# Modulation rows of a two-layer decoder trunk: row sums turned on VectorE, running sums pinned in the traced order, an earlier fold

## The chip, the cores and the metric

The kernel runs on one core of one Trainium2 chip. The metric is the device time of one execution in microseconds (us), as the median of several runs; lower is better. One execution is also recorded by the hardware profiler, and all rows below are from that one. Engines: PE is TensorE (matmul), PEld its weight loads, DVE is VectorE, ACT is ScalarE, POOL is GpSimd, SP is SyncE, which here only issues DMA transfers.

## The reference, cut to what matters

The trunk has two layers over a sequence of 512 tokens and a width D of 2048: first differential attention (8 heads), then forgetting attention (16 heads), which reads keys and values projected once from the first layer's output ("shared"). Each mixer reads its input modulated by a conditioning vector c:

```python
c_act = jax.nn.silu(c)                                   # 2048 numbers
mod = c_act @ w_mod[l] + b_mod[l]                        # 2048 x 6144 for each layer
shift, scale, gate = jnp.split(mod, 3, axis=-1)
h = x * (1.0 + scale[:, None]) + shift[:, None]
y = diff_attention(h, ...)                               # layer 0; forgetting_attention in layer 1
x = layer_norm(DN_ALPHA * x + gate[:, None] * y, ln_g[l], ln_b[l])
# between the layers, for the shared keys and values:
mod = c_act @ w_mod_kv + b_mod_kv                        # 2048 x 4096
shift, scale = jnp.split(mod, 2, axis=-1)
hk = x * (1.0 + scale[:, None]) + shift[:, None]
```

The change concerns the rows `c_act @ w` that are not needed at the start: the gate of layer 0, shift and scale of the shared projection ("kv"), and shift, scale and gate of layer 1, which are six rows of 2048 numbers.

## The kernel before, in words

**Projections.** All big products are done as three products of float32r parts (a value is split into a rounded "high" part and the remainder, "low"; `products`, lines 171 to 175: high x high, high x low, low x high). `group` (line 302) makes one projection of 512 columns: it holds four PSUM banks (`acc`), walks over 8 weight tiles, and for each tile issues four "bursts", one for each bank, of 6 matmuls with 512 moving columns. A `WeightStream` loads each weight tile (`wst`), ACT writes its high part (`whi`, line 93), DVE its low part (`wlo`, line 94), three tiles deep. When a bank's sum is complete, an `evac` function takes it out of PSUM through ACT and DVE; the next group writes the same bank.

**Order.** After each burst `tick` (line 286) runs one entry of the list `pieces` (a step of a head's attention, or nothing) and then, if the group's `bg` says so, takes the next step of a generator, `background`. The instructions are traced in this order. A scheduler then fixes the order on each engine when the context ends: it may move an instruction ahead of others traced before it, when its inputs are ready by the scheduler's own reckoning. Engines run their own instructions strictly in the order so fixed.

**Stages.** First comes a start stage (to about 200 us) with layer 0's own shift and scale and heads 0 and 1. Then come the groups of heads 2 to 7 in pairs: queries and keys (`qk[h]`), values and gate (`vg[h]`). While head h is projected, the attention of head h-1 runs as pieces: scores, softmax on DVE and ACT, transposes, values, and a norm that ends in `og` (line 758), whose transposes on PE are at line 772. The `evac` of a `vg` group writes `vl` (line 169) and `sg` (line 678). In `vg[7]` DVE also splits the finished heads into `hl`. Then the first output projection (`oA`, four groups of 512 columns), the shared values (`vj`) and keys (`kj`), layer 1's projections with its attention, and the second output projection.

**Later modulation.** `mod_stream` (line 353) is the generator in `background`. A row of 2048 numbers is made in four segments of 512 columns. For each segment 16 tiles of 128 x 512 weights are loaded (`ms`, two tiles to a 512 KB load, two buffers; in layer 1 single tiles `ms` and `msk`), and DVE adds them up: `macc = w * cact[:, kt] + macc`, one instruction for a step of the generator (line 387 for the first tile, 389 for the others), two `macc` buffers. That leaves 128 partial sums for each column, one for each partition, which must be added across partitions. `mod_row` (line 399) does that: ACT and DVE split `macc` into `mhi` and `mlo` (lines 168, 169), two PE matmuls with a matrix of ones as the stationary operand (lines 409, 410) add over the partitions into the bank `tr`, DVE adds the bias (`mrow`, line 411), and a DMA writes the 512 numbers to DRAM. The split is traced with tile 1 of the next segment, the matmuls with its tile 5. Segments 0 to 15 (line 633) run under the heads: gate of layer 0, kv shift, kv scale, layer 1's shift; 8 more (line 1106) under the shared projections. Steps are taken from `qk[3]` on (`bg=lambda k: k % 3 > 0`, then `k % 4 > 0`), one for each burst in the first `oA` group, and what is left in `open_n` (line 923).

**Fold.** `fold` (line 941) reads a finished pair of rows back from DRAM, turns it on PE (line 944) and merges it with the layer norm's parameters. For kv it is called in `open_n`, at the first bank's end in the first `oA` group.

Of the kernel before, what the change touches and what calls it, by code (L numbers as in the profile page):

```python
# [2 lines left out]

# [106 lines left out]
def tile_yoco(  # L110
# [50 lines left out]
    def tr_bank(name="tr"):  # L161
        return ps.tile([P, 512], F32, name=name, tag="tr", bufs=1)
# [4 lines left out]
    def split(hi, lo, src):  # L167
        S.copy(hi, src)
        V.tensor_tensor(lo, src, hi.bitcast(F32), op=ALU.subtract)
# [132 lines left out]
    def group(job, natural, evac, banks=range(4), bg=0, before_sub=None, after_sub=None, hold=0, after_held=None):  # L302


        acc = {b: acc_bank() for b in banks}
        w = job.width
        count = 0
        ns = KT // 2

        def burst(s, b, hi, lo):  # L310
            nonlocal count
            for kk in range(2):
                kt = 2 * s + kk
                bs = slice(b * P, (b + 1) * P)
                start, stop = kt == 0, kt == KT - 1
                if natural:
                    products(acc[b][:, :w], (Hh[kt][:, bs], Hl[kt][:, bs]), (hi[kk][:, :w], lo[kk][:, :w]), start, stop)
                else:
                    products(acc[b], (hi[kk][:, bs], lo[kk][:, bs]), (Hh[kt], Hl[kt]), start, stop)
            if s == ns - 1:  # L320
                evac(b, acc[b])
            tick(bg(count) if callable(bg) else bg)
            count += 1

        for s in range(ns - hold):
            if before_sub:
                before_sub(s)
            hi, lo = ws.get(job, s)
            for b in banks:
                burst(s, b, hi, lo)  # L330
            if after_sub:
                after_sub(s)
        for s in range(ns - hold + 3, ns):
            ws.advance(ws.where[(id(job), s)])

            pool, tag = (kpool, "K") if s < ns - hold + 5 else (hpool, "H")
            ws.step(lambda: pool.tile([P, 512], F32R, name="held", tag=tag))
# [15 lines left out]
    def mod_stream(segs, new_stage, new_acc, nk, deep=0, new_deep=None):  # L353

        todo = [(i, r) for i in range(len(segs)) for r in range(KT // nk)]
        loaded = {}
        summed = []

        def load(k):
            i, r = todo[k]
            src, col, _ = segs[i]
            t = new_deep() if k < deep else new_stage()
            rows = src[nk * r * P : nk * (r + 1) * P, col : col + 512]
            nc.sync.dma_start(t, rows.rearrange("(k p) n -> p k n", p=P) if nk > 1 else rows)
            loaded[k] = t

        def load_upto(k):
            n = len(loads)  # L370
            while n < len(todo) and n <= (k + 7 if n < deep else k + 2 // nk):
                load(n)
                loads.append(n)
                n += 1

        loads = []
        load_upto(-1)
        for k, (i, r) in enumerate(todo):
            load_upto(k)
            if r == 0:  # L380
                acc = new_acc()
            t = loaded.pop(k)
            for kk in range(nk):
                kt = nk * r + kk
                w = t[:, kk, :] if nk > 1 else t
                if kt == 0:
                    V.tensor_scalar(acc, w, cact[:, 0:1], None, op0=ALU.mult)
                else:
                    V.scalar_tensor_tensor(acc, w, cact[:, kt : kt + 1], acc, op0=ALU.mult, op1=ALU.add)  # L389
                if kt == KT - 1:  # L390
                    summed.append(segs[i][2](acc))
                if kt in (1, 5) and summed:
                    if next(summed[0], None) is None:
                        summed.pop()
                yield
        for _ in summed[0]:
            yield

    def mod_row(pool, ones_r, dst, bias, one):

        def steps(acc):
            hi = pool.tile([P, 512], F32R, name="mhi", tag="mhi", bufs=1)
            lo = pool.tile([P, 512], F32R, name="mlo", tag="mlo", bufs=1)
            split(hi, lo, acc)
            row = pool.tile([1, 512], F32, name="mrow", tag="mrow", bufs=1)
            nc.sync.dma_start(row, bias.rearrange("(o n) -> o n", o=1))
            yield True
            pt = tr_bank()
            PE.matmul(pt, ones_r, hi, start=True, stop=False)
            PE.matmul(pt, ones_r, lo, start=False, stop=True)  # L410
            V.scalar_tensor_tensor(row, pt[0:1, :], one, row, op0=ALU.add, op1=ALU.add)
            nc.sync.dma_start(dst, row)
        return steps


# [212 lines left out]
    actx = ExitStack()  # L628
    ap = actx.enter_context(tc.tile_pool(name="ap", bufs=1, reuse_waits="tile"))
    segs = []  # L630
    ones_a = ap.tile([P, P], F32R, name="ones_a")
    S.copy(ones_a, ones)
    for dst, src, col, bias, one in (
        (gate_dram[0], w_mod[0], 2 * D, b_mod[0], 0.0),
        (mod_dram[0][0:1, :], kv_w_mod, 0, kv_b_mod, 0.0),
        (mod_dram[0][1:2, :], kv_w_mod, D, kv_b_mod, 1.0),
        (mod_dram[1][0:1, :], w_mod[1], 0, b_mod[1], 0.0),
    ):
        for f0 in range(0, D, 512):
            cs = slice(col + f0, col + f0 + 512)  # L640
            segs.append((src, col + f0, mod_row(ap, ones_a, dst[:, f0 : f0 + 512], bias[cs], one)))
    background = mod_stream(
        segs,
        lambda: ap.tile([P, 2, 512], F32, name="ms", tag="ms", bufs=2),
# [160 lines left out]
    def keep(key, acc):  # L805
        raw[key] = kpool.tile([P, T], F32, name="raw", tag="K")
        S.copy(raw[key], acc)
# [6 lines left out]
    def split_og(kts):  # L814
        for kt in kts:
            new_h(kt)
            split(Hh[kt], Hl[kt], ogT[kt])
# [2 lines left out]
    drain()  # L820
    pieces.append(lambda_columns)
    pieces.extend(attention_a(0, 2))
    group(qk[2], False, lambda b, acc: keep(("qk", b), acc))
    drain()
    pieces.extend(first_qk(1))
    pieces.append(lambda: evac_qk(1)(3, raw["k1"]))
# [4 lines left out]
            drain()  # L831
        keep(b, acc)

    group(vg[2], True, keep_vg)
    for h in range(3, A_HEADS):

        first_steps, rest = attention_a(h - 1, spread=True)
# [28 lines left out]
    def ktile(name):  # L866
        return kpool.tile([P, T], F32, name=name, tag="K")
# [55 lines left out]
    def open_n():  # L923
        for _ in background:
            pass
        ab["kv"] = fold(0, ktile("mrow"))
        actx.close()
        pool = nctx.enter_context(tc.tile_pool(name="npool", bufs=1, reuse_waits="tile"))
        zp.extend((pool, pool.tile([P, TB, D], F32, name="n"), pool.tile([P, TB, 4, 6], F32, name="nstats")))
# [11 lines left out]
    def fold(k, row):  # L941
        nc.sync.dma_start(row[0 : 2 * KT, 0:P], mod_dram[k].rearrange("v (a p) -> (v a) p", p=P))
        pt = tr_bank()
        PE.transpose(pt[:, 0 : 2 * KT], row[0 : 2 * KT, 0:P], ident[0 : 2 * KT, 0 : 2 * KT])
        a1, b1 = cols(f"mod_a{k}"), cols(f"mod_b{k}")
        V.tensor_tensor(b1, pt[:, KT : 2 * KT], bncol, op=ALU.mult)
        V.tensor_tensor(b1, pt[:, 0:KT], b1, op=ALU.add)
        V.tensor_tensor(a1, pt[:, KT : 2 * KT], gcol, op=ALU.mult)
        return a1, b1
# [40 lines left out]
    def build_next(n=1):  # L990
        for _ in range(n):
            unit = next(built, None)
            if unit:
                build_half(unit[1], unit[0])

    pieces.extend(attention_a(A_HEADS - 1, 1))
    pieces.append(lambda: split_og((14, 15)))
    out_projection(oA, 0, zp, open_n, residual_a, norm_a, lambda b, k: build_next() if b == 3 and k < 2 else None)
    npool, n, nstats = zp

# [99 lines left out]
            ws.advance(ws.where[id(vj[0]), s] + 4)  # L1100
    forget = [forget_logits(q) for q in range(4)] + [None, forget_sums] + [None] * 8 + [columns_of_f]
    pieces.extend(forget)
    ones_b = npool.tile([P, P], F32R, name="ones_b")
    S.copy(ones_b, ones)
    segs = []
    for dst, col, one in ((mod_dram[1][1:2, :], D, 1.0), (gate_dram[1], 2 * D, 0.0)):
        for f0 in range(0, D, 512):
            cs = slice(col + f0, col + f0 + 512)
            segs.append((w_mod[1], col + f0, mod_row(npool, ones_b, dst[:, f0 : f0 + 512], b_mod[1, cs], one)))
    background = mod_stream(  # L1110
        segs,
        lambda: npool.tile([P, 512], F32, name="ms", tag="ms", bufs=3),
# [248 lines left out]
```

## Time and profile before

| what | value |
|---|---|
| median of 3 runs | 2004.19 us (2004.13 to 2004.77) |
| the profiled execution's own time | 2006.42 us |
| its span in the profile | 2004.4 us |
| granted TensorE clock, mean | 0.995 of full speed |
| instructions | 24916 |
| ACT busy | 720.3 us (36%) |
| read from HBM | 329.51 MB, 171 GB/s over the span |
| SP's longest kind of wait: `wst` load for a free buffer (DVE `wlo`) | 687.3 us in 208 waits |

The page gives each engine's busy time, the span in 40 slices of about 50 us, the costliest groups of instructions with the mean duration of one and the idle time ahead of it, and the chain of work that ended last. Other views list who waited for whom, single instructions in order of time, and sums over chosen stretches. A PE matmul's record is longer than the distance between two starts, since matmuls are pipelined: what a matmul takes from the others is the distance between starts. SP's waits are no loss in themselves, since a load issued early can only wait for its buffer.

### The profile page before, as it was taken

To read this page: it belongs to the slowest core of one execution; us is meant where nothing else is said; L and a number is where in the kernel's file an instruction comes from. 1 tells how busy PE (TensorE), PEld (TensorE's weight loads), DVE (VectorE), ACT (ScalarE), POOL (GpSimd) and SP (SyncE) were. 2 spreads that over 40 slices of the span, in tenths; PEclk is the share of its full clock that TensorE was granted. 3 is DMA by queue.
4 is the path that set the end of the run, shared out by engine and by line. 5 is a ranking of instruction groups with operands and counts; after the bars stand their busy time and mean duration, and the time that the engine had idled before them with its cause. 6 is when DMAs were issued, how large, how long until landed. Compare 5 with 4: busy or idle time off the path is not lost.

```text
span 2004.4 us, 24916 instructions
## 1 busy us (share of the span) xinstructions
PE 1963.8 (98%) x9115; PEld 1625.9 (81%) x9115; DVE 1317.3 (66%) x2398; ACT 720.3 (36%) x1235; POOL 2.2 (0%) x10
## 2 busy tenths in 40 slices
PE   5999999999999999999999999999999999999997
PEld 4888878888888888788888888888888888888886
DVE  6887865677777778853476666635455555576657
ACT  2432445333333334431263223224343333453123
POOL 0000000000000000000000000000000000000000
PEclk8999999999999999999999999999999999999999
DMA  9994742375757666452346788633323323233622
GB/s 339 348 315 147 243 151 85 106 231 186 224 178 231 189 219 211 164 166 95 116 147 215 238 272 268 226 95 126 102 93 103 98 94 101 95 115 99 229 93 105
DMA packets 258165, 343.81 MB, mean 172 GB/s; under 512 B 17702, under 2 KB 162492, under 8 KB 257276
## 3 DMA queue, kind: packets, MB, share of 16 engines
q1 hardware_dynamic: 255664, 338.02, 51.9%
q10 hardware_dynamic: 2380, 4.21, 0.6%
q8 instruction: 71, 1.16, 0.2%
q14 instruction: 50, 0.41, 0.1%
HBM read 329.51 MB, written 12.66 MB: 171 GB/s over the span
## 4 chain that ended last, share of the span: by engine, by line
PE 87%; DVE 6%; DMA 5%; SPq 1%; issue 1%; ACT 0%; DVEq 0%; ACTq 0%
PE acc L173 25%; PE acc L175 25%; PE acc L174 25%; DMA ms<-in_w_mod_dram 3%; PE sc L174 2%; PE sc L175 2%; PE sc L173 2%; DVE wlo L94 1%; PE o L175 1%; DVE macc L389 1%; PE o L174 1%; PE o L173 1%; DMA sms<-in_w_mod_dram 1%; PE tr L1213 1%; SPq L452 1%
## 5 line engine op out<-in xcount | busy, mean ns | idle before, releaser
L94 DVE TENSOR_TENSOR wlo<-wst,whi 128x1024 fp32r<-128x1024 f32 (+2 forms) x322 | 384.3, 1195 | 283.6 <-ACT whi L93 275.2
L93 ACT CAST whi<-wst 128x1024 fp32r<-128x1024 f32 (+2 forms) x322 | 331.6, 1030 | 637.5 <-PE acc L175 327.6
L173 PE MATMUL acc<-whi,hh 128*128 128x512 f32 x1232 | 483.6, 396 | 2.8 <-DVE sg L678 1.7
L174 PE MATMUL acc<-wlo,hh 128*128 128x512 f32 x1232 | 481.1, 390 | 0.1
L175 PE MATMUL acc<-whi,hl 128*128 128x512 f32 x1232 | 480.3, 390 | 0.0
L173 PE MATMUL acc<-hh,whi 128*128 128x512 f32 x1184 | 470.5, 397 | 1.0 <-DVE sg L678 1.0
L175 PE MATMUL acc<-hh,wlo 128*128 128x512 f32 x1184 | 462.3, 390 | 0.0
L174 PE MATMUL acc<-hl,whi 128*128 128x512 f32 x1184 | 462.2, 390 | 0.0
L389 DVE SCALAR_TENSOR_TENSOR macc<-ms,cact,macc 128x512 f32<-128x512 f32 x300 | 225.0, 750 | 87.0 <-DMA ms<-in_w_mod_dram 61.8
L173 PEld LDWEIGHTS acc<-whi,hh 128*128 128x128 f32 x1232 | 231.9, 188 | 49.9 <-DVE ztmp L909 1.6
L175 PEld LDWEIGHTS acc<-whi,hl 128*128 128x128 f32 x1232 | 231.5, 188 | 49.7
L174 PEld LDWEIGHTS acc<-wlo,hh 128*128 128x128 f32 x1232 | 231.7, 188 | 45.6 <-DVE wlo L94 0.5
L175 PEld LDWEIGHTS acc<-hh,wlo 128*128 128x128 f32 x1184 | 222.3, 188 | 48.6
L173 PEld LDWEIGHTS acc<-hh,whi 128*128 128x128 f32 x1184 | 222.6, 188 | 43.6 <-PE acc L175 1.4
L174 PEld LDWEIGHTS acc<-hl,whi 128*128 128x128 f32 x1184 | 222.8, 188 | 39.3
L479 DVE SCALAR_TENSOR_TENSOR sacc<-sms,cact,sacc 128x512 f32<-128x512 f32 (+1 forms) x127 | 89.5, 705 | 5.9 <-DMA sms<-in_w_mod_dram 2.3
L708 ACT ACTIVATE e<-e,mn 128x128 f32<-128x128 f32 (+3 forms) x64 | 36.1, 564 | 129.1 <-DVE mn L704 128.9
L1202 ACT ACTIVATE eb<-eb,mnb 128x128 f32<-128x128 f32 (+1 forms) x64 | 36.1, 564 | 95.6 <-DVE mnb L1199 94.5
L1199 DVE CUSTOM_DVE_ANT_0 eb<-sc,biasb 128x128 f32<-128x128 f32 (+1 forms) x64 | 31.4, 491 | 55.5 <-PE sc L175 55.5
L389 DVE SCALAR_TENSOR_TENSOR macc<-msk,cact,macc 128x512 f32<-128x512 f32 x60 | 44.5, 749 | 16.1 <-DMA msk<-in_w_mod_dram 14.9
L1217 DVE TENSOR_TENSOR pTl<-tr,pTh 128x128 fp32r<-128x128 f32 (+1 forms) x64 | 31.2, 488 | 25.2 <-ACT pTh L1216 24.8
L704 DVE CUSTOM_DVE_ANT_0 e<-sc,bias 128x128 f32<-128x128 f32 (+3 forms) x64 | 31.1, 486 | 20.9 <-PE sc L175 20.8
(267 smaller groups left out, 1805.9 us busy)
## 6 DMA issues: line engine op xcount, KB each, us to landing
wst<-in_a_w_in_dram SPq DMA_DIRECT2D x240, 256.0 KB
ms<-in_w_mod_dram SPq DMA_DIRECT2D x64, 512.0 KB
ms<-in_kv_w_mod_dram SPq DMA_DIRECT2D x64, 512.0 KB
wst<-in_kv_w_dram SPq DMA_DIRECT2D x64, 512.0 KB
wst<-in_b_w_in_dram SPq DMA_DIRECT2D x128, 256.0 KB
sms<-in_w_mod_dram SPq DMA_DIRECT2D x56, 512.0 KB
wst<-in_a_w_out_dram SPq DMA_DIRECT2D x32, 512.0 KB
msk<-in_w_mod_dram SPq DMA_DIRECT2D x64, 256.0 KB
```

The lines of the kernel that those rows point to most:

```text
L93: self.nc.scalar.copy(hi[:, :, :w], st[:, :, :w])
L94: self.nc.vector.tensor_tensor(lo[:, :, :w], st[:, :, :w], hi[:, :, :w].bitcast(F32), op=ALU.subtract)
L173: PE.matmul(dst, lhs[0], rhs[0], start=start, stop=False)
L174: PE.matmul(dst, lhs[0], rhs[1], start=False, stop=False)
L175: PE.matmul(dst, lhs[1], rhs[0], start=False, stop=stop)
L389: V.scalar_tensor_tensor(acc, w, cact[:, kt : kt + 1], acc, op0=ALU.mult, op1=ALU.add)
L479: V.scalar_tensor_tensor(acc, w, sc, acc, op0=ALU.mult, op1=ALU.add)
L704: V.tensor_tensor_reduce(out=e[:, :w], in0=sc[:, :w], in1=st["bias"][:, (3 - i) * P :], scale=-1.0, scalar=3.0e38, op0=ALU.add, op1=ALU.mi ...
L708: S.activation(e[:, :w], e[:, :w], AF.Exp, bias=mn, scale=-1.0, accum_out=rs)
L1199: V.tensor_tensor_reduce(out=e[:, :w], in0=sc[:, :w], in1=bias[:, :w], scale=-1.0, scalar=3.0e38, op0=ALU.add, op1=ALU.min, accum_out=mn)
L1202: S.activation(e[:, :w], e[:, :w], AF.Exp, bias=mn, scale=-1.0, accum_out=rs)
L1217: V.tensor_tensor(pTl[:, 0 : i + 1, ts], src, pTh[:, 0 : i + 1, ts].bitcast(F32), op=ALU.subtract)
```

## The change: what it does

1. **Row sums.** `mod_rows` takes the place of `mod_row`. For each segment DVE turns `macc` within blocks of 32 x 32 (`mturn`) and adds over the 32 turned columns of each block (`tensor_reduce`), which leaves 16 columns of `mred`: for each of the four groups of 32 partitions, the sums of that group. After the fourth segment one PE matmul in plain float32 with `mred` (128 x 64) as stationary operand and four identities of 32 x 32 stacked (`fours`) as moving operand adds the four groups: 64 x 32 numbers, the whole row. The bias is loaded and the row stored as 64 pieces of 32 numbers, once for a row and not once for a segment. ACT's `mhi`, DVE's `mlo` and the two matmuls of each segment are gone; ACT makes `fours` with four small copies, twice.
2. **Pinned sums.** Each `macc` instruction is passed to `keep_in_program_order`, which ties it behind the DVE instruction traced before it. It sets issue order alone, with no wait for that instruction's end. Instructions traced later may still be put ahead of it.
3. **Earlier steps.** `qk[2]` and `vg[2]` take steps of the generator too: 10 and 16.
4. **Fold.** The kv fold is a piece behind head 7's last steps and no longer in `open_n`.

In the order that the scheduler makes of it, the first `macc` stands in DVE's queue behind the `neglam` instruction (line 239) that is written during `qk[2]`; before, 22 `macc` instructions and the first `mlo` stood ahead of that one. The last row sum under the heads stands on PE about 200 matmuls earlier than before, and the kv fold's transpose 40 matmuls earlier.

```diff
@@ mod_stream
                 if kt == 0:
-                    V.tensor_scalar(acc, w, cact[:, 0:1], None, op0=ALU.mult)
+                    ins = V.tensor_scalar(acc, w, cact[:, 0:1], None, op0=ALU.mult)
                 else:
-                    V.scalar_tensor_tensor(acc, w, cact[:, kt : kt + 1], acc, op0=ALU.mult, op1=ALU.add)
+                    ins = V.scalar_tensor_tensor(acc, w, cact[:, kt : kt + 1], acc, op0=ALU.mult, op1=ALU.add)
+                tc.keep_in_program_order(ins)
@@
-    def mod_row(pool, ones_r, dst, bias, one):
-
-        def steps(acc):
-            hi = pool.tile([P, 512], F32R, name="mhi", tag="mhi", bufs=1)
-            lo = pool.tile([P, 512], F32R, name="mlo", tag="mlo", bufs=1)
-            split(hi, lo, acc)
-            row = pool.tile([1, 512], F32, name="mrow", tag="mrow", bufs=1)
-            nc.sync.dma_start(row, bias.rearrange("(o n) -> o n", o=1))
+    def four_ones(pool):
+
+        t = pool.tile([P, P], F32, name="fours", tag="fours")
+        for k in range(0, P, 32):
+            S.copy(t[k : k + 32, 0:32], ident[k : k + 32, k : k + 32])
+        return t[:, 0:32]
+
+    def mod_rows(pool, fours, dst, bias, one):
+
+        red = []
+
+        def steps(n, acc):
+            if n == 0:
+                red.append(pool.tile([P, 64], F32, name="mred", tag="mred", bufs=2))
+            t = pool.tile([P, 512], F32, name="mturn", tag="mturn", bufs=1)
+            V.transpose(t, acc)
+            V.tensor_reduce(
+                red[0][:, 16 * n : 16 * n + 16], t.rearrange("p (j q) -> p j q", q=32), axis=mybir.AxisListType.X, op=ALU.add
+            )
+            if n == 3:
+                row = pool.tile([64, 32], F32, name="mrow", tag="mrow", bufs=1)
+                nc.sync.dma_start(row, bias.rearrange("(j q) -> j q", q=32))
             yield True
-            pt = tr_bank()
-            PE.matmul(pt, ones_r, hi, start=True, stop=False)
-            PE.matmul(pt, ones_r, lo, start=False, stop=True)
-            V.scalar_tensor_tensor(row, pt[0:1, :], one, row, op0=ALU.add, op1=ALU.add)
-            nc.sync.dma_start(dst, row)
+            if n == 3:
+                pt = tr_bank()
+                PE.matmul(pt[0:64, 0:32], red[0], fours, start=True, stop=True)
+                V.scalar_tensor_tensor(row, pt[0:64, 0:32], one, row, op0=ALU.add, op1=ALU.add)
+                nc.sync.dma_start(dst.rearrange("o (j q) -> (o j) q", q=32), row)
         return steps
@@ segments (the same in layer 1's part with npool)
-    ones_a = ap.tile([P, P], F32R, name="ones_a")
-    S.copy(ones_a, ones)
+    fours = four_ones(ap)
...
-        for f0 in range(0, D, 512):
-            cs = slice(col + f0, col + f0 + 512)
-            segs.append((src, col + f0, mod_row(ap, ones_a, dst[:, f0 : f0 + 512], bias[cs], one)))
+        steps = mod_rows(ap, fours, dst, bias[col : col + D], one)
+        segs += [(src, col + 512 * f, partial(steps, f)) for f in range(4)]
@@
-    group(qk[2], False, lambda b, acc: keep(("qk", b), acc))
+    group(qk[2], False, lambda b, acc: keep(("qk", b), acc), bg=lambda k: k % 3 == 2)
@@
-    group(vg[2], True, keep_vg)
+    group(vg[2], True, keep_vg, bg=lambda k: k % 2)
@@ open_n
         for _ in background:
             pass
-        ab["kv"] = fold(0, ktile("mrow"))
         actx.close()
@@
     pieces.append(lambda: split_og((14, 15)))
+    pieces.append(lambda: ab.update(kv=fold(0, ktile("mrow"))))
     out_projection(oA, 0, zp, open_n, residual_a, norm_a, lambda b, k: build_next() if b == 3 and k < 2 else None)
```

More of the change, by code (lines that the diff above doesn't have):

```diff
@@ L2 @@
 from contextlib import ExitStack
+from functools import partial
 import concourse.bass as bass
@@ L1102, in tile_yoco @@
     pieces.extend(forget)
-    ones_b = npool.tile([P, P], F32R, name="ones_b")
-    S.copy(ones_b, ones)
+    fours = four_ones(npool)
     segs = []
     for dst, col, one in ((mod_dram[1][1:2, :], D, 1.0), (gate_dram[1], 2 * D, 0.0)):
-        for f0 in range(0, D, 512):
-            cs = slice(col + f0, col + f0 + 512)
-            segs.append((w_mod[1], col + f0, mod_row(npool, ones_b, dst[:, f0 : f0 + 512], b_mod[1, cs], one)))
+        steps = mod_rows(npool, fours, dst, b_mod[1, col : col + D], one)
+        segs += [(w_mod[1], col + 512 * f, partial(steps, f)) for f in range(4)]
     background = mod_stream(
```

## The prediction, made before the changed kernel ran

> **What bounds the kernel now.** I read the page's first two parts, then the sums by stretch, then who waits for whom on PE.
>
> ```profile
> PE 1963.8 (98%) x9115; PEld 1625.9 (81%) x9115; DVE 1317.3 (66%) x2398; ACT 720.3 (36%) x1235; POOL 2.2 (0%) x10
> ...
> PE   5999999999999999999999999999999999999997
> ```
>
> ```profile
> core 0: us, PE busy (x) PEld busy (x) DVE busy (x) ACT busy (x) POOL busy (x), PEclk, DMA share, GB/s
> ...
> 200.00:300.00 100.00, 97.68 (x464) 80.44 (x463) 76.38 (x169) 44.63 (x96) 0.00 (x0) 1.00 0.62 198
> 300.00:870.00 570.00, 566.83 (x2682) 470.80 (x2681) 413.20 (x861) 222.93 (x451) 0.00 (x0) 1.00 0.58 183
> ...
> 1060.00:1400.00 340.00, 340.00 (x1501) 280.47 (x1500) 206.29 (x265) 102.05 (x128) 0.00 (x0) 1.00 0.64 211
> ```
>
> PE sets the end: it is busy in 39 of 40 slices to 90% or more. The change works at 200 to 870 us (heads 2 to 7) and 1060 to 1400 us (shared projections). In the first, PE's records leave 2.3 + 3.2 = 5.5 us idle; in the second none. DVE is busy 489.6 of 670 us in the first stretch, so 180 us of its time are free. So two things can move the time: PE work that goes or comes, and the few stops of PE. A record says only that PE has something in flight, so I check the pace at the starts.
>
> ```profile
> 386.64 0.39 PE L175 MATMUL acc<-whi,hl 128*128 128x512 f32 x1
> 386.87 0.40 PE L409 MATMUL tr<-mhi,ones_a 128*128 128x512 f32 x1
> 387.10 0.40 PE L410 MATMUL tr<-mlo,ones_a 128*128 128x512 f32 x1
> 387.34 0.40 PE L173 MATMUL acc<-whi,hh 128*128 128x512 f32 x1
> ```
>
> A matmul of 512 columns takes its 0.23 us although its record lasts 0.39, at a granted clock of 1.00. The pair of the old row sum stands in that train like any other: from 386.87 to 387.34 it takes 0.47 us.
>
> **Part 1: the row sums.** How many go:
>
> ```profile
> L409 PE MATMUL tr<-mhi,ones_a 128*128 128x512 f32 x16 | 6.4, 399 | 0.0
> ...
> L409 PE MATMUL tr<-mhi,ones_b 128*128 128x512 f32 x8 | 3.2, 397 | 0.0
> ```
>
> 24 pairs at 0.47 us are 11.3 us, all on the path: **minus 11.3**. The Trainium skill, "TensorE: Matmul & The Clock Gate", Part 1, puts starts of back-to-back matmuls N / 2.4 GHz + about 2.5 ns apart, 0.216 us here; an estimate by that page is 48 x 0.216 = 10.4 us. The trace has 0.23, and the sum goes by the trace.
>
> Six float32 matmuls come, 64 columns of weights and 32 moving columns. The trace has none of this shape. The nearest of the kind (plain float32, shown as two records) is line 237; the other bound is the transpose at line 944, which also moves 32 columns:
>
> ```profile
> 223.93 0.40 PE L175 MATMUL acc<-hh,wlo 128*128 128x512 f32 x1
> 224.17 0.28 PE L237 MATMUL tr<-lam,ones 128*128 128x2 f32 x2
> 224.31 0.48 PE L173 MATMUL acc<-hh,whi 128*128 128x512 f32 x1
> 224.63 0.40 PE L174 MATMUL acc<-hl,whi 128*128 128x512 f32 x1
> ```
>
> ```profile
> 881.13 0.39 PE L175 MATMUL acc<-whi,hl 128*128 128x512 f32 x1
> 881.45 0.24 PE L944 MATMUL tr<-ident,mrow 32*128 32x32 f32 x1
> 881.62 0.50 PE L173 MATMUL acc<-whi,hh 128*128 128x512 f32 x1
> 881.96 0.40 PE L174 MATMUL acc<-wlo,hh 128*128 128x512 f32 x1
> ```
>
> Line 237 pushes the train back by 224.63 - 223.93 - 2 x 0.23 = 0.24 us, line 944 by 881.96 - 881.13 - 0.46 = 0.37. Six of them are 1.4 to 2.2; I take **plus 1.5**, near line 237, the same operation. So PE's work falls by 9.8 us (9.1 to 9.9).
>
> On DVE and ACT:
>
> ```profile
> L389 DVE SCALAR_TENSOR_TENSOR macc<-ms,cact,macc 128x512 f32<-128x512 f32 x300 | 225.0, 750 | 87.0 <-DMA ms<-in_w_mod_dram 61.8 <-DMA ms<-in_kv_w_mod_dram 19.9 <-DVE macc L389 0.3
> ...
> L411 DVE SCALAR_TENSOR_TENSOR mrow<-tr,mrow 1x512 f32<-1x512 f32 x24 | 16.2, 676 | 17.2 <-PE tr L410 14.9 <-DMA wst<-in_a_w_in_dram 2.3
> L169 DVE TENSOR_TENSOR mlo<-macc,mhi 128x512 fp32r<-128x512 f32 x24 | 16.2, 674 | 0.7 <-ACT mhi L168 0.7
> ...
> L911 DVE BATCH_NORM_STATS2 nstats<-n 128x6 f32<-128x512 f32 x16 | 10.4, 685 | 0.1
> ...
> L632 ACT CAST ones_a<-ones 128x128 fp32r<-128x128 f32 x1 | 0.3, 288 | 0.0
> ```
>
> DVE loses 24 x (0.674 + 0.676) = 32.4 us and gets 24 turns and 24 reductions over 128 x 512, and six small additions. The trace has neither operation; the nearest, a statistic that reads 512 columns and writes 6, takes 0.685. At that price the pair costs 1.37, as much as what it replaces; at twice the price (upper bound, an operation at half rate) it costs 1.4 us more for each segment, 22 us over the 16 under the heads, against 180 us free. I take no change: DVE's free time hides it, and if it stood ahead of an urgent instruction it would show as a stop of PE (below). The Trainium skill, "VectorE: DVE Perf Modes", Rules for kernel authors, speaks against this part: it calls `tensor_reduce` the slowest VectorE operation and advises against it on a hot path. No run here shows one yet; even at the double price above it would be off the path. ACT loses its 24 `mhi` and gets 8 copies of 32 x 32, at most 0.29 each by `ones_a`; it is busy under 45% in both stretches, so 0. SP issues 12 small transfers for 48, and the bias and result rows go in 64 pieces; each is needed tens of us later: 0.
>
> **Parts 2 and 3: where the running sums stand.** PE's stops between 200 and 870 us, by the waits:
>
> ```profile
> PE acc L173 <- DVE sg L678: 2.7, 3, 1.0
> PE tr L772 <- DVE og L758: 2.6, 3, 1.3
> ```
>
> What made DVE late is in the chain and on DVE's own line:
>
> ```profile
> 241.18 5.22 DMA ms<-in_w_mod_dram
> ...
> 263.76 4.71 DMA ms<-in_w_mod_dram
> ```
>
> ```profile
> 826.89 0.75 DVE L389 SCALAR_TENSOR_TENSOR macc<-ms,cact,macc 128x512 f32<-128x512 f32 x1 [1.08 <-DMA ms<-in_w_mod_dram]
> 827.56 0.41 DVE L678 SCALAR_TENSOR_TENSOR sg<-th,acc 128x256 f32<-128x256 f32 x1
> ```
>
> ```profile
> 257.71 0.41 PE L772 MATMUL tr<-ident,og 128*128 128x128 f32 x2 [1.26 <-DVE og L758]
> ...
> 273.89 0.41 PE L772 MATMUL tr<-ident,og 128*128 128x128 f32 x2 [0.85 <-DVE og L758]
> ...
> 333.73 0.41 PE L772 MATMUL tr<-ident,og 128*128 128x128 f32 x2 [0.50 <-DVE og L758]
> ...
> 728.00 0.47 PE L173 MATMUL acc<-hh,whi 128*128 128x512 f32 x1 [0.97 <-DVE sg L678]
> ...
> 828.12 0.47 PE L173 MATMUL acc<-whi,hh 128*128 128x512 f32 x1 [1.04 <-DVE sg L678]
> ...
> 832.24 0.47 PE L173 MATMUL acc<-whi,hh 128*128 128x512 f32 x1 [0.65 <-DVE sg L678]
> ```
>
> ```profile
> DVE macc L389 <- DMA ms<-in_w_mod_dram: 61.8, 50, 3.0
> ...
> DVE macc L389 <- DMA ms<-in_kv_w_mod_dram: 19.9, 23, 1.8
> ```
>
> A `macc` that was moved forward waits at DVE's head for its load, and the `og` or `sg` behind it makes PE wait. The built order of the changed kernel: between `neglam` and head 0's first `og` stand 5 sums where 14 stood, and none is early enough to outrun loads that the chain shows at about 5 us; in the end of `vg[7]` both first `sg` now stand ahead of the next `macc`. At 333.73 no `macc` stood near, so that wait of 0.50 stays. That leaves 5.3 - 0.5 = 4.8 us of idle records in five stops (two `og`, three `sg`). Each costs 0.39 - 0.23 = 0.16 more than its idle time, as the record of the matmul before runs on past its slot: 4.8 + 0.8 = 5.6. But 26 sums now stand in groups where the old ones had run ahead, and each pinned sum can still wait for its load (its 50 and 23 waits before cost PE only these stops). I set 1.5 us for new stops, about one at the size of the worst: **minus 4.1** (bounds: minus 6 with no new stop, plus 3 if two or three more come than go). The late half (1060 to 1400 us) has no stop to lose, and DVE is free for 134 of 340 us: 0.
>
> **Part 4: the fold.** PE reaches its transpose 40 matmuls (9 us) earlier, about 872 us. Its load:
>
> ```profile
> L942 SPq DMA_DIRECT2D mrow<-mod_dram x1: 457/457/457, 860.2 to 860.2; - x1
> ```
>
> It left at 860.2 and stands behind the same weight loads in SP's order; 12 us remain where the chain's loads took about 5, so 0. If that cover went, PE would stop once, for some us: inside the range.
>
> **Sum.** -11.3 + 1.5 - 4.1 = -13.9 us. Against the profiled execution that is a span of 2004.4 - 13.9 = 1990.5; its own time, 2006.4, is 2.2 above the median, which I take for the difference of a profiled run. From the median: 2004.2 - 13.9 = **1990.3 us**.
>
> **Rivals.**
>
> *The stops change places.* PE work falls by 9.8, but pinned sums ahead of other `og` and `sg` make as many stops as went: 2004.2 - 9.8 = 1994.4. For it: DVE stays as full, and the sums ask for the same loads in fewer places. Against it: between 334 and 728 us the sums ran steadily and the rows above have no stop. Chance 0.28, 1992.5 to 1997.
>
> *Slower: the sum at the head of the queue.* Pinned sums can no longer use a quiet stretch; before the end of each `qk` and `vg` group and each of two `og` of a head, DVE would wait for `ms` with the urgent instruction behind. Six heads have 24 such places; at the mean of the five stops (5.6 / 5 = 1.1 us) they cost 26 where 5.6 went: 2004.2 - 9.8 - 5.6 + 26.4 = 2015. It decides from 15.4 / 24 = 0.64 us a place on. Against it: 73 waits of `macc` for `ms` gave only five stops so far. Chance 0.04.
>
> *Turn and reduction far dearer than the rows.* If the pair takes several us in one piece ahead of an `evac`, about 12 group ends lose 0.3 to 1 us each: 1998 to 2003. Chance 0.06.
>
> *It does not do what it says.* If PE hid the 48 matmuls in idle slots, nothing would fall: 2004. The starts at 386.64 to 387.34 speak against it. Chance 0.02.
>
> **How the numbers follow.** The forecast (1987.5 to 1992.5) has 0.60, the rivals 0.28, 0.04, 0.06 and 0.02. The range from 1987.5 to 1997.0 holds the first two, 0.88, and I keep its ends, which are the bounds: -11.3 + 1.4 - 6 = -15.9 below, -9.8 + 3 above. A measurement of this kernel tells 0.2%, 4 us, from no change: faster is below 2000.2, slower above 2008.2. Faster 0.92 (0.60, 0.28 and two thirds of the 0.06), same 0.04, slower 0.04.
>
> **What would show it.** Right: no line 409 or 410; about 14 us less span, nearly 8 of it between 200 and 870 us from the row sums and 4 from stops; 3.5 us less at 1060 to 1400; PE's waits for `sg` and `og` down to about 2 us together; six small matmuls at 0.24 to 0.37 each; turn and reduction near 0.7 each. Wrong: waits of PE for `sg`, `og`, `k0l` or `wlo` that add to 5 us or more, a turn or reduction above 1.4 us, a stop at the fold, or waits for `wst` at PE's start.

## The result, and the profile after

| | before | after |
|---|---|---|
| median | 2004.86 us (6 runs, 2004.13 to 2007.21) | 1995.71 us (6 runs, 1992.9 to 1996.93) |
| ratio of the times, 95% interval | | 0.9955 (0.9944 to 0.9965) |
| the profiled execution: its own time, span | 2006.42, 2004.4 us | 1992.90, 1991.1 us |

The change saves 9.1 us by the medians; 13.9 were forecast. The two traces stand 13.3 us apart, but they are no typical pair. The trace of after is the quickest of its six executions. That of before lies near the upper end of its spread: in all there are 53 timed executions of the kernel before, from 2002.2 to 2007.3 us, and six of them are at 2006.42 or above.

The page of the changed kernel, its first two parts:

```profile
PE 1955.8 (98%) x9079; PEld 1618.8 (81%) x9079; DVE 1320.8 (66%) x2404; ACT 708.2 (36%) x1217; POOL 2.2 (0%) x10
...
PE   5999999999999999999999999999999999999997
```

PE still sets the end and is busy 8.0 us less. DVE is busy 3.5 us more, ACT 12.1 us less, mostly as 24 casts `mhi` went. Two of the stretches that were shown for before (PE, PEld, DVE, ACT, POOL, granted clock, DMA share, GB/s):

```profile
200.00:300.00 100.00, 100.00 (x479) 83.41 (x478) 65.36 (x154) 45.00 (x97) 0.00 (x0) 1.00 0.46 145
300.00:870.00 570.00, 567.90 (x2685) 469.85 (x2684) 439.11 (x908) 218.63 (x445) 0.00 (x0) 1.00 0.63 199
```

PE's records leave 2.1 us idle between 200 and 870 us where they left 5.5; in a second trace of the change (e3) they leave 3.2. Who PE waited for there in the first (us in all, times, longest):

```profile
PE acc L174 <- DVE sg L695: 1.6, 3, 0.6
PE tr L789 <- DVE og L775: 0.5, 1, 0.5
```

The new operations, in the two answers for the tiles `mturn` and `mred` (ns: least, median, most; first and last start in us):

```profile
L419 DVE STREAM_TRANSPOSE mturn<-macc x24: 700/710/714, 286.7 to 1341.9; 128x512 f32<-128x512 f32 x24
L420 DVE TENSOR_REDUCE mred<-mturn x24: 664/682/689, 287.4 to 1342.9; 128x16 f32<-128x512 f32 x24
```

```profile
L429 PE MATMUL tr<-fours,mred x12: 222/233/244, 425.8 to 1344.0; 128*64 128x32 f32 x12
```

Turn and reduction take 0.71 + 0.68 = 1.39 us, where the prediction took 1.37. The small matmul's record is short, but its price is what it does to the train around it (start, duration):

```profile
834.73 0.39 PE L176 MATMUL acc<-whi,hl 128*128 128x512 f32 x1
834.95 0.39 PE L174 MATMUL acc<-whi,hh 128*128 128x512 f32 x1
835.29 0.30 PE L429 MATMUL tr<-fours,mred 128*64 128x32 f32 x2
835.53 0.50 PE L175 MATMUL acc<-wlo,hh 128*128 128x512 f32 x1
835.87 0.39 PE L176 MATMUL acc<-whi,hl 128*128 128x512 f32 x1
836.10 0.40 PE L174 MATMUL acc<-whi,hh 128*128 128x512 f32 x1
836.33 0.39 PE L175 MATMUL acc<-wlo,hh 128*128 128x512 f32 x1
```

From 834.73 to 836.33 stand five matmuls of 512 columns (0.227 us each where nothing is between them) and the small one: 1.60 - 5 x 0.227 = 0.46 us for it. The other five places give 0.43 to 0.44. So six of them cost about 2.7 us, not 1.5.

### The profile page after: what moved, and what is told of

Read it like the earlier page. It is cut to its first block, busy times and chain, and to the rows that moved or that the text cites. A ratio compares the mean times of both kernels' runs of the same rounds, so it can differ in the third digit from the quotient of the medians.

```text
span 1991.1 us, 24748 instructions
## 1 busy us (share of the span) xinstructions
PE 1955.8 (98%) x9079; PEld 1618.8 (81%) x9079; DVE 1320.8 (66%) x2404; ACT 708.2 (36%) x1217; POOL 2.2 (0%) x10
## 4 chain that ended last, share of the span: by engine, by line
PE 91%; DVE 4%; DMA 2%; issue 1%; ACT 1%; SPq 0%; DVEq 0%; ACTq 0%
PE acc L174 26%; PE acc L176 26%; PE acc L175 26%; PE sc L174 2%; PE sc L175 2%; PE sc L176 2%; PE o L176 1%; PE o L174 1%; PE o L175 1%; PE tr L1228 1%; DMA ms<-in_w_mod_dram 1%; DVE wlo L95 1%; DMA ms<-in_kv_w_mod_dram 1%; DVE sacc L498 1%; DVE macc L391 1%
## 5 line engine op out<-in xcount | busy, mean ns | idle before, releaser
L1231 ACT CAST pTh<-tr 128x128 fp32r<-128x128 f32 (+1 forms) x64 | 27.2, 424 | 44.3 <-PE tr L1228 43.5
```

The costliest lines, as they stand in the source:

```text
L1231: S.copy(pTh[:, 0 : i + 1, ts], src)
```

## The experiments

Theory A: the gain is PE's work (48 matmuls less, six small ones more), and the order of the sums decides only how many stops PE has. Its rival B: a good part of the gain is stops that the pinned order takes away. The table has the medians; each kernel stands against executions of the kernel before that were timed beside it (2004.2 us for e1 to e4, 2004.83 for e5 to e8, 2005.18 for e9 to e12).

| run | what it has | median us | against before, us | ratio (95%) |
|---|---|---|---|---|
| e1_rows_alone | new row sums | 2015.76 | +11.6 | 1.0062 (1.0050 to 1.0075) |
| e2_order_alone | pins, early steps, earlier fold; old row sums | 2004.99 | +0.8 | 1.0003 (0.9994 to 1.0011) |
| e3_all_again | the whole change | 1994.31 | -9.9 | 0.9951 (0.9939 to 0.9964) |
| e4_no_pin | the change without pins | 2018.77 | +14.6 | 1.0075 (1.0061 to 1.0089) |
| e5_braked | new row sums, a small matmul for each segment; no pins | 2004.15 | -0.7 | 0.9997 (0.9988 to 1.0006) |
| e6_quiet_ends | the change, more early steps, no sums at the ends of `vg[3]` to `vg[7]` | 1995.44 | -9.4 | 0.9954 (0.9942 to 0.9967) |
| e7_no_early | the change without early steps | 2009.41 | +4.6 | 1.0029 (1.0018 to 1.0039) |
| e8_before_again | the kernel before, once more | 2002.47 | -2.4 | one run |
| e9_pair_back | the change, and the 48 matmuls as pure load | 2005.64 | +0.5 | 1.0003 (0.9994 to 1.0012) |
| e10_pins_alone | pins | 2017.67 | +12.5 | 1.0064 (1.0050 to 1.0077) |
| e11_fold_back | the change with the fold at its old place | 1995.34 | -9.8 | 0.9953 (0.9941 to 0.9966) |
| e12_more_early | the change with more early steps | 1994.38 | -10.8 | 0.9948 (0.9935 to 0.9960) |

### The parts alone

**e1_rows_alone**, as against the changed kernel:

```diff
-                tc.keep_in_program_order(ins)
-    group(qk[2], False, lambda b, acc: keep(("qk", b), acc), bg=lambda k: k % 3 == 2)
+    group(qk[2], False, lambda b, acc: keep(("qk", b), acc))
-    group(vg[2], True, keep_vg, bg=lambda k: k % 2)
+    group(vg[2], True, keep_vg)
+        ab["kv"] = fold(0, ktile("mrow"))
-    pieces.append(lambda: ab.update(kv=fold(0, ktile("mrow"))))
```

> Only the row sums are changed (turn, reduction, one small matmul for a row, one store for a row); the running sums are not pinned, heads 2's groups take no steps and the kv fold stays where it was. Theory A (the gain is PE's work alone, and the stops of PE that went are made up by others in a usual execution): 9.8 us less than before, about 1995.1 against 2004.9, ratio 0.9951. Theory B (the order of the sums is worth about 4 us in a usual execution, and the row sums bring less than their PE time): 5 us less, about 1999.9. By A the trace shows 48 matmuls fewer and PE's waits for sg and og stay at 4 to 6 us or go to other places.

**e2_order_alone**: the kernel before, with

```diff
+                tc.keep_in_program_order(ins)
+    group(qk[2], False, lambda b, acc: keep(("qk", b), acc), bg=lambda k: k % 3 == 2)
+    group(vg[2], True, keep_vg, bg=lambda k: k % 2)
-        ab["kv"] = fold(0, ktile("mrow"))
+    pieces.append(lambda: ab.update(kv=fold(0, ktile("mrow"))))
```

> The old row sums (48 matmuls with ones), but pinned running sums, the steps in head 2's groups and the earlier kv fold. Theory A: no change, 2004.9 within 1.5 us (ratio 0.9993 to 1.0007). Theory B: 4 us less, about 2000.8, ratio 0.998. The forecast on record would have it 4.1 less.

**e3_all_again**: the changed kernel once more, no edit.

> The changed kernel once more, for a second profiled execution and more timed ones. Both theories: median near 1995.7. If the profiled execution on record (span 1991.1) was an unusually quick one, this one's span is 1993 to 1995, and PE's waits for DVE between 200 and 870 us add to 3 to 6 us and not to 2.1. If it was usual, the span is again near 1991 and the timed runs are slower than profiled ones for another reason.

**e4_no_pin**: the changed kernel less one line.

```diff
-                tc.keep_in_program_order(ins)
```

> The changed kernel without the pins: new row sums, steps in head 2's groups, earlier fold, but the scheduler may move the running sums forward. Theory A: as the changed kernel, 1995.7 within 1.5. Theory B: the pins are the part that takes the stops away, so 4 us more, about 1999.7.

e3 has its median near the old one, with a span of 1992.5 us and 3.2 us of waits in its trace. Both theories missed e4: without the one line the kernel takes 2018.77 us, 24.5 more than e3, which was timed beside it.

The order alone gives nothing: +0.6 us by its ratio, -1.2 to +2.2 by the interval. That speaks for A. But the row sums alone, whose work on PE is less, are 11.6 us **slower** than before, and neither A nor B gives a reason for that. The sums and waits of e1 between 300 and 870 us:

```profile
300.00:870.00 570.00, 554.71 (x2601) 458.78 (x2600) 398.82 (x842) 207.90 (x427) 0.00 (x0) 0.99 0.55 174
```

```profile
PE acc L174 <- DVE sg L694: 6.7, 2, 3.5
PE acc L174 <- DVE q0l L676: 3.8, 3, 2.2
PE tr L788 <- DVE og L774: 2.2, 2, 1.4
```

PE is idle for 15.3 us there (3.2 before), behind DVE. Against before, that is 12.7 us more idle time between 200 and 870 us and 2.5 more between 870 and 1400; two of the stops also cost some 1.6 us each at a lower clock (last section). Less the 8.6 us of PE work that went, this makes about 10 of the 11.6 us. What DVE did ahead of the worst of these stops:

```profile
435.62 1.54 DVE L391 SCALAR_TENSOR_TENSOR macc<-ms,cact,macc 128x512 f32<-128x512 f32 x2 [1.01 <-DMA ms<-in_kv_w_mod_dram]
437.07 1.22 DVE L95 TENSOR_TENSOR wlo<-wst,whi 128x1024 fp32r<-128x1024 f32 x1
...
439.19 0.75 DVE L391 SCALAR_TENSOR_TENSOR macc<-ms,cact,macc 128x512 f32<-128x512 f32 x1 [0.57 <-DMA ms<-in_kv_w_mod_dram]
439.86 0.41 DVE L694 SCALAR_TENSOR_TENSOR sg<-th,acc 128x256 f32<-128x256 f32 x1
```

Running sums stand ahead of the urgent `sg`, two of them waiting for their loads. They stand there because the whole stream runs early. The running sums of the first layer in the kernel before, and in e1 (first and last start):

```profile
L389 DVE SCALAR_TENSOR_TENSOR macc<-ms,cact,macc x229: 730/752/754, 211.2 to 834.3; 128x512 f32<-128x512 f32 x115
```

```profile
L391 DVE SCALAR_TENSOR_TENSOR macc<-ms,cact,macc x230: 710/751/755, 199.9 to 675.6; 128x512 f32<-128x512 f32 x115
```

In e1 all 16 segments are done by 676 us, in e4 by 639, in the kernel before by 834; after the change they end at 833. The old row sums had a brake in them. `mhi` and `mlo` are single buffers that a matmul of PE reads, and PE's program has that matmul at its late place; the next segment can't be split before it. In e1 a turn is free as soon as the reduction on the same engine is done, so the scheduler lets the sums run ahead, into the busiest groups of DVE. This reading is tried next.

### The brake put back, and the pins by themselves

**e5_braked**: e1 with one small matmul and one store for each segment, and a single buffer that it reads.

```diff
+            red = pool.tile([P, 16], F32, name="mred", tag="mred", bufs=1)
+            V.tensor_reduce(red, t.rearrange("p (j q) -> p j q", q=32), axis=mybir.AxisListType.X, op=ALU.add)
...
             yield True
+            pt = tr_bank()
+            PE.matmul(pt[0:16, 0:32], red, fours, start=True, stop=True)
```

> The new row sums without pins, without steps in head 2's groups and with the old place of the fold, as in the run that changed the row sums alone, but with one small matmul and one store for each segment, and a single buffer for the 16 reduced columns. So every segment's reduction waits until PE has read the one before it at its traced place. Theory (the old pair of matmuls was a brake: its single buffers, read by PE in a late place, kept the scheduler from running the sums ahead, and without it the sums fill DVE's queue from 280 us on): PE's work falls by 24 x 0.47 - 24 x 0.25 = 5.3 us, stops as before, about 1999 against 2004.2, ratio 0.9975, and the twelfth segment's first sum starts near 600 us or later. Rival (turn and reduction themselves make DVE late, or the missing mhi on ACT shifts something): slow as without the brake, 2012 to 2016.

No pin, no early step, and the sums are held again:

```profile
L391 DVE SCALAR_TENSOR_TENSOR macc<-ms,cact,macc x229: 732/752/754, 211.2 to 803.6; 128x512 f32<-128x512 f32 x115
```

The fifth to eleventh segments begin at 390, 422, 455, 494, 526, 562 and 600 us; in the kernel before the fourth to tenth begin at 389, 421, 454, 493, 525, 561 and 599. So e5 keeps the old pace, one segment ahead. In e1 the fourth to tenth begin at 280, 305, 339, 367, 395, 423 and 450. The 11.6 us are gone, with the turn and the reduction still there and `mhi` still away. So the brake is shown: a reader on PE for each segment holds the sums, and without it, or pins in its stead, they cost more than the row sums save. (`mred` and `mrow` are both single buffers in e5; which of them holds was not tried.) That e5 is no quicker than before, where 1999 was expected, is mostly due to its 24 small matmuls. From 876.25 to 877.52 its train has four matmuls and one of them:

```profile
876.25 0.39 PE L175 MATMUL acc<-wlo,hh 128*128 128x512 f32 x1
876.47 0.39 PE L176 MATMUL acc<-whi,hl 128*128 128x512 f32 x1
876.79 0.23 PE L421 MATMUL tr<-fours,mred 128*16 128x32 f32 x2
876.95 0.50 PE L174 MATMUL acc<-whi,hh 128*128 128x512 f32 x1
877.29 0.39 PE L175 MATMUL acc<-wlo,hh 128*128 128x512 f32 x1
877.52 0.40 PE L176 MATMUL acc<-whi,hl 128*128 128x512 f32 x1
```

That is 1.27 - 4 x 0.227 = 0.36 us. 24 of these are 8.6 us of the 11.3 that the pairs took. That leaves a gain of 2.7, where 0.7 was measured (-2.4 to +1.2 by the interval): up to 2 us stay unexplained.

**e10_pins_alone**: the kernel before and one line more.

```diff
+                tc.keep_in_program_order(ins)
```

> The kernel before with only the line that keeps the running sums in program order. By the brake theory the old row sums already hold the running sums near their place in the program, so the pins alone change little by themselves; but without the early steps the last segments end late, as in the run of the changed kernel without them (1 stop of 7.8 us, +13.7). If that stop belongs to the late end of the stream, it comes here too, on the old pair: 2008 to 2018. If it belongs to the new small matmul alone, the pins alone give 2003 to 2006.

**e7_no_early**: the changed kernel without its early steps.

```diff
-    group(qk[2], False, lambda b, acc: keep(("qk", b), acc), bg=lambda k: k % 3 == 2)
+    group(qk[2], False, lambda b, acc: keep(("qk", b), acc))
-    group(vg[2], True, keep_vg, bg=lambda k: k % 2)
+    group(vg[2], True, keep_vg)
```

> The changed kernel without the steps in head 2's groups: the pinned sums begin with head 3's. If those 26 steps matter, the last sums and DVE's work crowd into the first output projection (26 sums and one turn more there) and 2 to 4 us come back, 1997 to 1999; if not, 1994 to 1996 as the changed kernel.

The first branch of e10's expectation held, on the old row sums too: +12.5 us. e7 itself had been expected at 1999 at most. Pinned sums that begin only with head 3 end late, at 889 us in e10 and 884 in e7, and the last row sum is then the one that PE waits for. The waits of e7 and of e10 between 850 and 920 us, one line of each:

```profile
PE tr L429 <- DVE mred L420: 7.8, 1, 7.8
```

```profile
PE tr L410 <- ACT mhi L168: 6.8, 1, 6.8
```

DVE in e7 ahead of it:

```profile
880.64 1.54 DVE L391 SCALAR_TENSOR_TENSOR macc<-ms,cact,macc 128x512 f32<-128x512 f32 x2 [1.89 <-DMA ms<-in_w_mod_dram]
...
885.57 0.69 DVE L420 TENSOR_REDUCE mred<-mturn 128x16 f32<-128x512 f32 x1
```

`open_n` runs out the stream, and each pair of sums stands for its load there while the matmul of the last row blocks PE's queue. The stop is 7.8 us, but e7 is 14.0 us slower than e6, timed beside it, and e6 is no different from the changed kernel. The rest is the clock (the seventh column is the granted one):

```profile
875.00:880.00 5.00, 3.59 (x16) 2.63 (x14) 2.44 (x5) 1.36 (x3) 0.00 (x0) 1.00 0.99 342
880.00:885.00 5.00, 0.00 (x0) 0.00 (x0) 4.26 (x6) 0.45 (x3) 0.00 (x0) 0.69 0.76 275
885.00:890.00 5.00, 2.73 (x8) 2.14 (x9) 4.39 (x9) 0.00 (x0) 0.00 (x0) 0.50 0.80 216
890.00:895.00 5.00, 5.00 (x19) 4.04 (x18) 4.82 (x9) 0.00 (x0) 0.00 (x0) 0.78 0.60 161
```

After PE's restart at 886.4, 2.73 us of work go at half the clock and 5.00 at 0.78: 1.4 + 1.1 = 2.5 us more. With a wait of 0.9 right after the stop, and one of 1.5 for `al` (the low part of the attention weights) that the changed kernel does not have, that is 12.7 of the 14.0 us.

### PE's work put back

**e9_pair_back**: the changed kernel, with the old pair at each segment's late step on constant operands that wait for nothing.

```diff
             yield True
+            pt = tr_bank()
+            PE.matmul(pt, pair[0], pair[1], start=True, stop=False)
+            PE.matmul(pt, pair[0], pair[1], start=False, stop=True)
```

> The changed kernel with the 48 ones-matmuls of the old row sums put back as pure load: two fp32r matmuls of 512 columns on constant operands at each segment's late step, which wait for no running sum and whose result nobody reads (the row sums are still made the new way). If PE's work is the whole gain of the change, as the run with the order alone says (0 of its 9 to 10 us), then 24 x 0.47 = 11.3 us come back: 2006.0 (1995.0 + 11.3), in the interval 2004 to 2008. If the gain came from stops that go with the pair (a pair that waits for its operand), the constant pair costs less than half of that: below 2001.

Measured 2005.64, 10.3 us above e11, timed beside it (and e11 is the changed kernel in all but the fold). The pair in the train:

```profile
502.30 0.39 PE L436 MATMUL tr<-pair_m,pair_w 128*128 128x512 f32 x1
502.53 0.39 PE L437 MATMUL tr<-pair_m,pair_w 128*128 128x512 f32 x1
502.75 0.39 PE L174 MATMUL acc<-whi,hh 128*128 128x512 f32 x1
```

It takes 502.75 - 502.30 = 0.45 us, and up to 0.47 at other undisturbed places: 10.8 to 11.3 in 24. The 10.3 us that came back are the whole gain, within the spread of the executions: the pair that waits for nothing costs as much as the old one did. That is A; what is left for B is bounded by e2, 1.2 us at the most.

### What is left of the stops

**e6_quiet_ends**: more early steps, and no sum after step 27 of the gated groups of heads 3 to 7.

```diff
+    group(qk[2], False, lambda b, acc: keep(("qk", b), acc), bg=lambda k: k % 3 > 0)
+    group(vg[2], True, keep_vg, bg=lambda k: k % 4 > 0)
+        group(vg[h], True, evac_rest, bg=lambda k: k < 28 and k % 4 > 0, after_sub=early if h == A_HEADS - 1 else None)
```

> The changed kernel, with more steps in head 2's groups (21 and 24 for 10 and 16) and none in the last four bursts of the v and gate groups of heads 3 to 7. Theory (the stops that are left, two to five waits for sg of 0.3 to 1 us, come from sums traced just ahead of an evac): those stops go, 2 to 3 us less than the changed kernel, about 1992 against 2004.2 for before, ratio 0.994. Rival (the stops come from DVE's load in these stretches whatever stands there, or from head 2's denser sums): no change or 1 to 2 us more than the changed kernel, 1994 to 1997.

**e8_before_again**: the kernel before, for a second trace of it.

> The kernel before once more, for a second profiled execution. The one on record was 2.2 us above the median of its kernel. If that was stops of PE that a usual execution doesn't have, this one shows a span near 2002.3 and waits of PE for sg and og between 200 and 870 us of about 3 us and not 5.3. If they are the same 5.3 us, the usual execution is shorter elsewhere.

**e12_more_early**: the first two lines of e6 alone.

> The changed kernel with more running sums in head 2's projections (two of three places in the first group, three of four in the second, for one of three and one of two), so that the stream ends earlier and head 7's groups end with fewer sums. If the two sg stops left at the end of head 7 (818 and 822 us, 1.0 us together) come from the stream's last sums, they go, and the time falls by 1 to 2 us to 1993 to 1994.5. If stops only change places, as with the quiet ends, it stays at 1994 to 1997; if DVE gets too full in head 2 it is slower, above 1998.

**e11_fold_back**: the changed kernel, the fold back at the end of the sums (in `open_n`).

> The changed kernel with the fold of the shared modulation at its old place, after the last running sum instead of among the last steps of head 7. My theory prices the fold at 0: 1993 to 1997, the changed kernel's own range. The rival, that the earlier fold took a wait off the start of the shared projections, gives 2 to 5 us more: 1997 to 2000.

e6 gives 1995.44, where 1992 was expected: the stops change places (its waits for `og` are 1.3 us, for `sg` 1.1, for `mrow` 0.8). e12 gives 1994.38; the two `sg` stops at the end of `vg[7]` are gone, as expected, and its waits for `sg` fall from the 2.6 of e11 to 0.6, while waits for `mrow` (0.7) and `mred` (0.3) come. It can't be told from the changed kernel (1995.71, 1994.31, and e11's 1995.34), so no version here beats it measurably. e11 shows no measurable worth of the fold, as forecast. And e8, at 2002.47, shows the kernel before with fewer stops in the same place:

```profile
PE tr L772 <- DVE og L758: 2.5, 3, 1.3
PE acc L173 <- DVE sg L678: 0.9, 2, 0.7
```

3.4 us, where the trace that the prediction read had 5.3.

## Why the prediction was right and wrong, step by step

| step | forecast us | measured us |
|---|---|---|
| 24 pairs of ones-matmuls | -11.3 | -10.3 (e9 against e11), -10.8 to -11.3 by its starts |
| six small matmuls | +1.5 (1.4 to 2.2) | +2.7 |
| stops of PE | -4.1 (-6 to +3) | +0.6 by e2's ratio (-1.2 to +2.2) |
| turn and reduction on DVE | 0 | 0; 1.39 us a pair, hidden, once the sums are held |
| ACT, SP, the fold | 0 | 0 (e11 for the fold) |
| sum | -13.9 | -9.1 (e3: -9.9) |

PE's work comes to -10.8 + 2.7 = -8.1 by the starts (-8.6 with the 0.47 of the prediction's rows). The 0.5 to 1.8 us from there to -9.1 and -9.9 fit in e2's interval and can't be assigned more closely.

The direction and the largest term were right. The measured 1995.7 lies above the forecast's own part of the range (1987.5 to 1992.5), in the part that belongs to the first rival. That the row sums came together with pins and early steps was luck as far as the sum goes: it gave the row sums 9.8 us of gain whatever the order, and alone they cost 11.6.

- **The pairs: right.** They stood in the train, not in idle slots; e9 brings them back and the time with them.
- **"I take plus 1.5, near line 237, the same operation": wrong,** and outside its bounds. Both neighbours were too cheap. Line 944 is one record, where plain float32 runs as two. Line 237 has two, but it moves 2 columns and not 32, and its weight load (PEld) runs ahead, under the matmul before it: it starts at 223.94 for a matmul at 224.17. The load of the new matmul starts only with it, at all six places, as that of line 944 does. One line of before, one of after:

```profile
223.94 0.42 PEld L237 LDWEIGHTS tr<-lam,ones 128*128 128x128 f32 x2
```

```profile
835.29 0.19 PEld L429 LDWEIGHTS tr<-fours,mred 128*64 128x64 f32 x2 [0.38 <-DVE mred L420]
```

So from the start of the matmul ahead to the new one pass 0.32 to 0.34 us, where the train takes 0.23 and line 237 took 0.24. To the next start it takes another 0.24 (0.16 with 16 columns of weights in e5, 0.14 for line 237). Why the load does not run ahead was not tried.

- **"Minus 4.1": the step that failed.** Of the five stops that were counted, the two of `og` and the one at 728 us are gone in all three traces of the change. The two at the end of `vg[7]` stayed: 0.37 and 0.64 us in after, 0.97 and 0.66 in e3, 1.05 and 0.64 in e11, where before had 1.04 and 0.65. The first `sg` there does stand ahead of the next `macc`, as the prediction says, but other work of DVE stands ahead of it:

```profile
816.53 1.22 DVE L95 TENSOR_TENSOR wlo<-wst,whi 128x1024 fp32r<-128x1024 f32 x1
...
818.00 0.68 DVE L170 TENSOR_TENSOR hl<-ogT,hh 128x512 fp32r<-128x512 f32 x1
818.60 0.41 DVE L695 SCALAR_TENSOR_TENSOR sg<-th,acc 128x256 f32<-128x256 f32 x1
```

The second of them stood behind a `wlo` of 1.22 us in before already (DVE at 830.54), and still does. New stops come near 529 us, 0.6 to 0.9 us together. And the price came from a single execution, 2.2 us above the median. A second trace of before has 3.4 us of waits in place of 5.3; the traces of the change have 2.1 (after), 3.2 (e3) and 3.1 (e11). So 0.2 to 3.2 us of idle time go between one trace and another, and the medians of e2 see none of it.

- **"2.2 above the median, which I take for the difference of a profiled run": wrong.** The profiled execution of e2 is 1.9 us under its kernel's median, that of after 2.8 under, that of before 1.6 above the median of its six timed ones. They are executions like the others. The two traces of before differ by 3.7 us in span and by 1.9 in idle time between 200 and 870 us: about half of the difference is stops of the kind that was counted as gain.
- **DVE's free time hides the new pair: right for this kernel, for a reason that the prediction didn't have.** The sum treated the row sums and the order as independent. They are not: the row sums alone cost 11.6 us, the pins alone 12.5, and both together without the early steps 4.6. The 180 us of free time of DVE did not help e1, as its sums stood where DVE was full.
- **The rivals.** "The stops change places", 1994.4, is nearest to what came. "The sum at the head of the queue", 2015, does not come with pins; e1 has it without them, for the opposite cause, as sums that are not held run into the groups' ends.
- **Two slips that changed nothing.** PE is busy to 90% or more in 38 of the 40 slices, not 39. And the bounds of the sum, -15.9 and -6.8, give 1988.3 and 1997.4; the ends of the range were 1987.5 and 1997.0.
- **The Trainium skill** ("VectorE: DVE Perf Modes", Rules for kernel authors) calls `tensor_reduce` the slowest operation of VectorE. Here it takes 0.682 us for 128 x 512 float32, the turn 0.710 and a running sum over the same tile 0.747: it isn't slower than its neighbours, and it is off the path.

## What to carry to other kernels

An operation that you remove may be what kept a scheduler's filler work at its place: look for single buffers that another engine reads late, and measure the removal alone before you take the other parts for small additions. A gain read from stops of half an us each needs more than one trace of the kernel before, and a check of what stands ahead of the late instruction at each of them, while work on the engine that is full can be priced from the starts in one train. A shape that the trace lacks is not bounded by its two nearest rows if they differ from it in what makes the price: compare the number of records, the columns that are moved, and whether the weight load runs ahead of the matmul.

## What the runs showed of the hardware

The longest stops of PE cost more than their length. The worst of e1:

```profile
436.34 0.39 PE L175 MATMUL acc<-wlo,hh 128*128 128x512 f32 x1
436.57 0.39 PE L176 MATMUL acc<-whi,hl 128*128 128x512 f32 x1
440.43 0.47 PE L174 MATMUL acc<-hh,whi 128*128 128x512 f32 x1 [3.47 <-DVE sg L694]
...
442.62 0.63 PE L174 MATMUL acc<-hh,whi 128*128 128x512 f32 x1
443.04 0.63 PE L175 MATMUL acc<-hl,whi 128*128 128x512 f32 x1
...
444.61 0.39 PE L176 MATMUL acc<-hh,wlo 128*128 128x512 f32 x1
444.83 0.39 PE L174 MATMUL acc<-hh,whi 128*128 128x512 f32 x1
```

Before the stop the starts are 0.23 apart, at 442 to 444 us 0.43, and from 444.6 on 0.22 again: about 3.3 us at half pace, some 1.6 us lost on top of the 3.5. The granted clock of e1 between 440 and 445 us is 0.66. The other long stop of e1, 3.23 us up to 545.88, did the same: the granted clock is 0.68 between 545 and 550 us. No stop of up to 2.4 us between 200 and 870 us did that. The longest is one of 2.38 us in e4, up to 541.12, and the clock of e4 is 1.00 from 540 to 550 us. The Trainium skill, "TensorE: Matmul & The Clock Gate", Part 1, says that the clock falls to half after an idle window of about 3.4 us and comes back after one of sustained work. The stops of 3.47, 6.8 and 7.8 us agree with it (the granted clock is 0.50 between 885 and 890 us of e7, and between 890 and 895 of e10); the one of 3.23 us lies a little under that figure.
